# One more seven-product chunk in the second column half of an output projection

## The chip, the cores and the metric

The kernel runs on one core of a Trainium2 chip. The metric is the device time of one execution in microseconds (us). The engines are TensorE (PE, with its weight loads shown as PEld), VectorE (DVE), ScalarE (ACT), GpSimd (POOL) and SyncE (SP); SP and POOL issue the DMAs.

## The reference

One decoder layer on 256 tokens with model width 2048, all in float32:

```python
proj = h @ w_in[l]                                   # q, k, v of 16 heads of 128
a_out = diff_attention(q_d, k_d, v_d, ...)           # 8 heads, two 64-wide sub-heads each
b_out = moba_attention(q_m, k_m, v_m, cos_m, sin_m)  # 8 heads; 256 tokens are one block
mix = jnp.concatenate([a_out, b_out], axis=-1) @ w_out[l]
h = layer_norm(DEEPNORM_ALPHA * h + mix, ln1_g[l], ln1_b[l])
f = conv_ffn(h, w_up[l], conv_w[l], conv_b[l], w_down[l])   # width 5632
h = layer_norm(DEEPNORM_ALPHA * h + f, ln2_g[l], ln2_b[l])
```

The change touches `@ w_out` (2048 x 2048), its preparation during the attention, and the first `layer_norm`.

## The kernel before

**Stages.** Weights are streamed once, in items of a `stream` list, and the order of every engine's work is the order in which the code is written. There are 16 items for v, 32 for q and k (a q item and a k item for each head, called steps 0 to 31 here, counted from `first_q`), 16 for the output projection (from `first_o`; steps 32 to 47 in the same count), then 88 for gate and up, then the down projection. Each weight tile is loaded as float32 (`raw`, by SP at L179), then split into a rounded part `hi` (ACT, L203) and a remainder `lo` (DVE, L205; some remainders go by ACT L201 and a POOL DMA L202). A product of blocks is three matmuls: hi with hi, lo with hi, hi with lo. All of these are recorded at L303.

**Attention steps.** For each head there are: the Square of the previous head's output and its scale (`out_norm`: ACT L482, DVE L483 `ss`, POOL L484, then ACT L491), the scores' maxima (`scores`: DVE L412, and L416 `nm`), the exponentials (`exps`: ACT L426), the probabilities (`probs`: DVE L434 `rs` to L441), and on PE the transposes of the probabilities (`probs_t`: L450). The transposes stand in PE's queue between the q and k matmuls.

**Output projection.** The columns are handled in two halves (`half` 0 and 1), each with eight chunks `j` of 256 rows of `w_out`. A chunk is eight block products for its two row blocks and two token blocks, or 24 matmuls of 128x512. Some chunks use a Strassen-like scheme of seven products, or 21 matmuls. Its weight sums are either made on the spot (`mm_seven`; in half 0 chunk 6, in half 1 chunk 3), or made ahead (`mm_ready`; the list `READY`). Both also need sums of the two activation blocks (`act_sums` on DVE, `act_sums_split` on ACT and DVE). In half 0 chunks 3, 5 and 4 are in `READY`; two chunks of the down projection (`"d"`) are there as well. The second of these, `APART`, has its own tiles.

**Sums made ahead.** `READY_AT` gives five steps for each chunk: the DMA load of the weights into `prep` tiles (`ready_load`, SP, L832 or L835), two pairs of DVE sums (`ready_sums`: L852 and L853, then L855 and L856), and two remainders (`ready_lo`: DVE L881). Half a step behind each pair of sums stands the rounding (`ready_hi`: ACT L875), and half a step behind each remainder the store of both parts to a DRAM tile `tsums` (`ready_store`: POOL L888, L889). The chunk `STAYS` is kept on the chip and isn't stored. Before the output projection needs a stored chunk, `ready_fetch` loads it into `oslot`. These calls are put into the stream's steps behind the attention's own, by `pending`. All chunks share two `prep` tiles in turn: the load of chunk c goes into the tile of the second sums of chunk c-1.

**Around the projection's end.** `o_shared` adds the products that several outputs share into `z` (DVE L1286), `z_piece` adds a finished bank to `z` and takes its statistics (L518, L521), `normed` normalises a piece of `z` (L1346), and PE transposes it (L1355). The first matmuls of gate and up need the transposed pieces.

```python
READY_AT = ((0, 3, 5, 7, 9), (8.5, 11, 13, 15, 17), (17.5, 20, 21, 22, 23), (23.5, 26, 27, 29, 34.5), (2.5, 5, 9, 13, 17))
...
for step, fn, j in ((x, ready_load, ()), (u[0], ready_sums, (0,)), (u[0] + 0.5, ready_hi, (0,)),
                    (u[1], ready_sums, (1,)), (u[1] + 0.5, ready_hi, (1,)), (u[2], ready_lo, (0,)),
                    (u[2] + 0.5, ready_store, (0,)), (u[3], ready_lo, (1,)), (u[3] + 0.5, ready_store, (1,))):
```

Of the kernel before, what the change touches and what calls it, by code (L numbers as in the profile page):

```python
# [11 lines left out]
F32 = mybir.dt.float32  # L12
# [4 lines left out]
P = 128  # L17
D = 2048
# [39 lines left out]
STAYS, APART = 3, 4  # L58

ORDER = {"v": (1, 0, 2, 3), "d": (0, 1, 2, 3), "o": (2, 0, 1, 3)}  # L60

# [18 lines left out]
def hymba_layer(ctx: ExitStack, tc: tile.TileContext, a: dict):  # L80
# [25 lines left out]
        stream.append(("q", h, 0, a["w_qk"][h, 0]))  # L106
        stream.append(("k", h, 0, a["w_qk"][h, 1]))
    for half in range(2):
        for j in range(8):
            stream.append(("o", half, j, a["w_o"][half, j]))  # L110
    for f in range(FT):

# [518 lines left out]


    gap = []

    def act_sums(i):
        kind, p, _, _ = stream[i]
        if kind == "d":
            return
        if kind == "o":
            j = 2 * stream[i][2]  # L640
            if "hraw" not in kept:
                kept["hraw"] = keep.tile([P, 4, S], F32, name="hraw", tag="four")
                kept["hsum"] = [keep.tile([P, S], F32R, name=n, tag=t) for n, t in (("hh", "cos_m"), ("hl", "sin_m"))]
            x = kept["hraw"][:, 0:2]
            both = [heads[k, j // NDIFF][:, j % NDIFF:j % NDIFF + 2].bitcast(F32) for k in range(2)]
            DVE.tensor_tensor(x, *both, ALU.add)
# [177 lines left out]
    def ready_load(c):  # L824
        if c == 0:
            ready["w"] = [keep.tile([P, 2048], F32, name="prep", tag=x) for x in ("za", "zb")]
            ready["dram"] = dram.tile([len(READY), P, 8, 512], F32R, name="tsums")
        if c == APART:
            ready["apart"] = [keep.tile([P, 2048], F32, name="apart", tag=x) for x in ("mab", "mbb")]
        kind, p, n = READY[c]  # L830
        if kind == "o":
            SP.dma_start(ready_half(c, 0), a["w_o"][p, n])  # L832
            return
        for k in range(2):
            SP.dma_start(ready_half(c, 0)[:, k * 1024:k * 1024 + 1024],  # L835
                         a["w_d"][2 * p + 1 - k][:, n * 1024:(n + 1) * 1024])
# [435 lines left out]
    def o_shared(n, part):  # L1272

        if part == 0:
            kept["ou"] = [work.tile([P, 512], F32, name="tf", tag="m1") for _ in range(2)]
            kept["ou"].append(work.tile([P, 512], F32, name="u", tag="sh", bufs=1))
        a, b, c = kept["ou"]
        if part == 0:
            ACT.activation(a, MO[n][1], AF.Copy)
            DVE.tensor_tensor(b, MO[n][6], a, ALU.add)  # L1280
            DVE.tensor_tensor(c, MO[n][7], b, ALU.add)
        adds = (((0, 1, MO[n][5], ALPHA), (1, 1, MO[n][5], ALPHA), (0, 0, a, ALPHA)) if part == 0 else
                ((0, 1, b, 1.0), (1, 0, c, ALPHA), (1, 1, c, 1.0)))
        for t, c, src, alpha in adds:
            y = z[:, t, (2 * n + c) * 512:(2 * n + c + 1) * 512]
            DVE.scalar_tensor_tensor(y, y, alpha, src, op0=ALU.mult, op1=ALU.add)  # L1286

    last = range(first_u - PAIRED, first_u)
    for i in range(first_o, last[0]):
# [4 lines left out]
        if i == last[0] - 1:  # L1294
            both = Two(*(keep.tile([P, 2, 1024], F32R, name="both", tag=x) for x in ("biga", "bigb")), 2)
            split(first_u + 1, 0, both)
            split(first_u + 1, 1, both)
        if i == first_o:
            oslot()
            ready_fetch(first_o + 3, [kept["oslot"][:, 0:8]], POOL)  # L1300
        if seven(i) or ready_of(i) is not None:
            for kk in range(2):
                aparts[i, kk] = head(0, 2 * stream[i][2] + kk), head(1, 2 * stream[i][2] + kk)
            if seven(i):
                mm_seven(i)
            else:
                mm_ready(i, (1, 2, 3, 4, 5, 7, 6))
        elif i == last[0] - 1:
            for kk in range(2):
                mm_o(i, kk, 0)  # L1310
        else:
            if not ahead:
                mm_o(i, 0, 1)
            mm_o(i, 0, 0)
            if ahead:
                mm_o(i, 1, 1)
            middle(i)
# [4 lines left out]
        n, j = stream[i][1:3]
        if i == first_o + 1:
            z0 = keep.tile([P, 1, D], F32, name="z", tag="za")
# [707 lines left out]
```

## Time and profile before

| | |
|---|---|
| median of 3 runs | 1100.79 us (1100.35 to 1100.85) |
| profiled execution, its own time | 1100.75 us |
| span of that execution | 1099.0 us |
| PE busy | 1092.2 us (99%) |
| DVE busy | 964.9 us (88%) |
| ACT busy | 739.5 us (67%) |
| bytes moved | 305.86 MB |

The span is the time from the first to the last instruction; the execution's own time is 1.75 us longer. All instants below are us from the span's start. A row of the trace gives the start, the duration, the engine, the line, the operation, its output and inputs, and, in square brackets, how long the engine had been idle before it and what ended that. A q or k step lasts about 6.4 us (the second chunk's sums, of steps 11 and 13, start at 161.22 and 174.05 us), and the output projection runs from about 300 us to 387 us.

### The profile page before, as it was taken

To read this page: it belongs to the slowest core of one execution; us is meant where nothing else is said; L and a number is where in the kernel's file an instruction comes from. 1 tells how busy PE (TensorE), PEld (TensorE's weight loads), DVE (VectorE), ACT (ScalarE), POOL (GpSimd) and SP (SyncE) were. 2 spreads that over 40 slices of the span, in tenths; PEclk is the share of its full clock that TensorE was granted. 3 is DMA by queue.
4 is the path that set the end of the run, shared out by engine and by line. 5 is a ranking of instruction groups with operands and counts; after the bars stand their busy time and mean duration, and the time that the engine had idled before them with its cause. 6 is when DMAs were issued, how large, how long until landed. Compare 5 with 4: busy or idle time off the path is not lost.

```text
span 1099.0 us, 16343 instructions
## 1 busy us (share of the span) xinstructions
PE 1092.2 (99%) x5879; PEld 942.4 (86%) x5879; DVE 964.9 (88%) x1652; ACT 739.5 (67%) x1199; POOL 88.2 (8%) x125
## 2 busy tenths in 40 slices
PE   9999999999999999999999999999999999999998
PEld 6888888888888898888888888888888888888886
DVE  6988899898789979888999989998899988999887
ACT  5766677766556586666666767676776767777563
POOL 0100111110000000000000000000000001000003
PEclk9999999999999999999999999999999999999999
DMA  9888898988788557988988889898898899888683
GB/s 328 275 279 270 271 328 271 321 257 261 248 321 259 206 204 228 290 275 267 310 278 287 282 295 335 295 316 296 278 275 282 316 317 293 290 286 266 232 323 123
DMA packets 73082, 305.86 MB, mean 278 GB/s; under 512 B 7604, under 2 KB 9640, under 8 KB 54440
## 3 DMA queue, kind: packets, MB, share of 16 engines
q1 hardware_dynamic: 58168, 242.67, 59.5%
q0 software_dynamic: 14400, 59.78, 23.0%
q10 hardware_dynamic: 432, 2.36, 0.6%
q8 instruction: 46, 0.75, 0.3%
q14 instruction: 36, 0.29, 0.1%
HBM read 245.49 MB, written 28.84 MB: 250 GB/s over the span
## 4 chain that ended last, share of the span: by engine, by line
PE 99%; DMA 0%; ACT 0%; SPq 0%; issue 0%; ACTq 0%
PE bank L303 98%; PE bank L450 0%; DMA raw<-in_w_v 0%; PE bank L1355 0%; PE bank L497 0%; ACT z L1961 0%; ACT hi L235 0%; PE bank L1394 0%; ACT z L1957 0%; SPq L165 0%; SPq L250 0%; PE bank L1946 0%; ACTq L1957 0%
## 5 line engine op out<-in xcount | busy, mean ns | idle before, releaser
L303 PE MATMUL bank<-h,hi 128*128 128x512 f32 x1376 | 480.9, 391 | 0.0
L303 PE MATMUL bank<-h,lo 128*128 128x256 f32 x1376 | 388.1, 282 | 0.0
L303 PEld LDWEIGHTS bank<-h,hi 128*128 128x128 f32 x1376 | 258.3, 188 | 54.3
L303 PEld LDWEIGHTS bank<-h,lo 128*128 128x128 f32 x1376 | 260.2, 189 | 3.7
L223 DVE TENSOR_TENSOR lo<-raw,hi 128x1024 fp32r<-128x1024 f32 x175 | 211.8, 1214 | 13.0 <-ACT hi L215 12.4
L215 ACT ACTIVATE hi<-raw 128x1024 fp32r<-128x1024 f32 x175 | 181.9, 1043 | 6.9 <-PE bank L303 6.9
L303 PE MATMUL bank<-x,hi 128*128 128x512 f32 x512 | 183.0, 398 | 0.0
L203 ACT ACTIVATE hi<-raw 128x1024 fp32r<-128x1024 f32 x121 | 124.9, 1045 | 33.6 <-PE bank L303 17.4
L205 DVE TENSOR_TENSOR lo<-raw,hi 128x1024 fp32r<-128x1024 f32 x105 | 124.3, 1206 | 24.1 <-ACT hi L203 23.8
L303 PE MATMUL bank<-x,lo 128*128 128x256 f32 x512 | 144.3, 282 | 0.0
L1014 ACT ACTIVATE tslot<-tf 128x512 fp32r<-128x512 f32 x144 | 88.7, 627 | 61.9 <-DVE tf L1676 27.0
L303 PEld LDWEIGHTS bank<-x,hi 128*128 128x128 f32 x512 | 96.2, 188 | 20.5 <-issue 1.0
L1017 DVE TENSOR_TENSOR tslot<-tf,tslot 128x512 fp32r<-128x512 f32 x144 | 97.7, 688 | 11.4 <-ACT tslot L1014 10.5
L1481 ACT ACTIVATE ub<-bank 128x512 f32<-128x512 f32 x86 | 50.8, 591 | 72.0 <-PE bank L303 71.9
L303 PEld LDWEIGHTS bank<-x,lo 128*128 128x128 f32 x512 | 96.8, 189 | 0.2
L303 PE MATMUL bank<-hi,x 128*128 128x512 f32 x192 | 51.7, 391 | 0.6 <-ACT hi L235 0.6
L1622 POOL DMA_DIRECT2D rslot<-raw x17 | 14.9, 879 | 436.9 <-ACT sp L1020 436.9
L303 PE MATMUL bank<-tslot,more 128*128 128x512 f32 x192 | 49.1, 391 | 0.0
L591 ACT ACTIVATE gc<-ub,vec 128x256 f32<-128x256 f32 x43 | 25.8, 599 | 30.9 <-DVE ub L1490 30.9
L1490 DVE TENSOR_TENSOR ub<-ub 128x256 f32<-128x256 f32 x86 | 36.2, 420 | 11.8 <-ACT ub L1481 11.8
L303 PE MATMUL bank<-tslot,sp 128*128 128x512 f32 x180 | 45.0, 391 | 0.0
L303 PEld LDWEIGHTS bank<-hi,x 128*128 128x128 f32 x192 | 35.8, 188 | 8.8 <-ACT hi L235 1.5
(354 smaller groups left out, 1739.4 us busy)
## 6 DMA issues: line engine op xcount, KB each, us to landing
raw<-in_w_u SPq DMA_DIRECT2D x88, 1024.0 KB, 6.9
raw<-in_w_qk SPq DMA_DIRECT2D x32, 1024.0 KB, 6.2
raw<-in_w_d SPq DMA_DIRECT2D x48, 512.0 KB, 8.6
rows<-in_w_d SPq DMA_DIRECT2D x38, 512.0 KB, 5.1
raw<-in_w_v SPq DMA_DIRECT2D x28, 512.0 KB, 8.9
raw<-in_w_o SPq DMA_DIRECT2D x13, 1024.0 KB, 7.8
rslot<-raw POOLq DMA_DIRECT2D x17, 768.0 KB, 7.0
dparts<-rslot SPq DMA_DIRECT2D x38, 256.0 KB, 8.1
```

The lines of the kernel that those rows point to most:

```text
L203: ACT.activation(hi[:, s], t[:, x:y], AF.Copy)
L205: DVE.tensor_tensor(lo[:, s], t[:, x:y], hi[:, s].bitcast(F32), ALU.subtract)
L215: ACT.activation(hi[:, 0:w], t[:, half * 1024:half * 1024 + w], AF.Copy)
L223: DVE.tensor_tensor(lo[:, 0:w], t[:, half * 1024:half * 1024 + w], hi[:, 0:w].bitcast(F32), ALU.subtract)
L303: PE.matmul(out, lhsT, rhs, start=start, stop=stop)
L591: ACT.activation(gates[f], g, AF.Identity, bias=vec[:, C_CB + f:C_CB + f + 1], scale=vec[:, C_W + 2 * FT + f:C_W + 2 * FT + f + 1])
L1014: ACT.activation(side["t"][:, 0, j], f, AF.Copy)
L1017: DVE.tensor_tensor(side["t"][:, 1, j], f, side["t"][:, 0, j].bitcast(F32), ALU.subtract)
L1481: ACT.activation(t.rearrange("p j t -> p (j t)"), up_bank(i), AF.Copy)
L1490: DVE.tensor_tensor(u[:, 0], u[:, 0], u[:, 1], ALU.add)
L1622: POOL.dma_start(side["r"][:, 1], w[:, 0:3], accum_op=ALU.add)
```

## The change

A sixth chunk, `("o", 1, 5)`, joins `READY`: chunk 5 of half 1 now takes seven products by `mm_ready` and no longer eight. In half 1 it is worked ahead of chunk 4 rather than behind it (`O_ORDER`). The sums of the activations of chunks 3 and 5, which half 0 makes, stay in their tiles (`held`) and are used again in half 1, so `act_sums` does nothing there. These sums are written in smaller pieces (128x256 and 128x128 rather than 128x512 and 128x256), and in other tiles. In `READY_AT` the chunks stand closer: the second chunk's sums move from steps 11 and 13 to 10.5 and 12, its remainders from 15 and 17 to 13.5 and 15; the third chunk's load moves from 17.5 to 15.5 and its first sums from 20 to 17; the new chunk takes 21.5 to 26, and `STAYS` starts at 27.5 rather than 23.5. Weights for the prepared `"o"` chunks are loaded in two DMAs rather than one, except for `STAYS`. The new chunk's sums are fetched in four DMAs of 0.5 MB at `first_o + 7`. Two of the six `z` additions of half 1 (`o_shared(1, 1)`) move behind the first token half's `normed`, and a remainder split of the next stage moves between two `z_piece` calls.

```diff
-READY = (("o", 0, 3), ("o", 0, 5), ("d", PT - 2, 0), ("o", 0, 4), ("d", PT - 1, 0))
+READY = (("o", 0, 3), ("o", 0, 5), ("d", PT - 2, 0), ("o", 1, 5), ("o", 0, 4), ("d", PT - 1, 0))
-READY_AT = ((0, 3, 5, 7, 9), (8.5, 11, 13, 15, 17), (17.5, 20, 21, 22, 23), (23.5, 26, 27, 29, 34.5), (2.5, 5, 9, 13, 17))
+READY_AT = ((0, 3, 5, 7, 9), (8.5, 10.5, 12, 13.5, 15), (15.5, 17, 18, 19, 20), (21.5, 23.5, 24.5, 25, 26),
+            (27.5, 29.5, 31, 30.5, 34.5), (2.5, 5, 9, 13, 17))
+SUMS_AT = ((5, 0), (5, 1), (4, 0), (6, 0))
+O_ORDER = (range(8), (0, 1, 2, 3, 5, 4, 6, 7))
...
     def act_sums(i):
+        if kind == "o" and p == 1:
+            sums[i] = held[n]
+            return
...
-            SP.dma_start(ready_half(c, 0), a["w_o"][p, n])
+            for x, y in ((1024, 2048), (0, 1024)) if c != STAYS else ((0, 2048),):
+                SP.dma_start(ready_half(c, 0)[:, x:y], a["w_o"][p, n][:, x:y])
...
-    for j, step in enumerate((first_q + 28, first_o + 2.5)):
+    for j, step in enumerate((first_q + 30, first_o + 2.5)):
         extra.setdefault(step, []).insert(0, (ready_here, (j, "hi")))
...
-        adds = (((0, 1, MO[n][5], ALPHA), (1, 1, MO[n][5], ALPHA), (0, 0, a, ALPHA)) if part == 0 else
-                ((0, 1, b, 1.0), (1, 0, c, ALPHA), (1, 1, c, 1.0)))
+        adds = (((0, 1, MO[n][5], ALPHA), (1, 1, MO[n][5], ALPHA), (0, 0, a, ALPHA), (0, 1, b, 1.0)) if part == 0 else
+                ((1, 0, c, ALPHA), (1, 1, c, 1.0)))
...
-            split(first_u + 1, 1, both)
...
-            for part in range(2):
+            for part in range(2 - n):
                 at(i + 1 + part / 2, o_shared, n, part, rank=0)
         if i == first_o + 7:
             SP.dma_start(z[:, 1, 1024:], a["x"][:, 1, 1024:])
+            ready_fetch(first_o + 12, [kept["oslot"][:, 8:16]])
...
     z_piece(0, 2, bank[4], 1, 512, 1.0)
+    split(first_u + 1, 1, both)
...
     for c in range(4):
         normed(0, mv, rstd, c)
+    o_shared(1, 1)
     for j in range(2):
         split_lo(first_u, j)
```

Below, the same places in the order of the instructions, with the line numbers of each kernel; in the changed kernel they are 4 to 12 higher (L875 is L884 there, L482 is L486, L426 is L430, L881 is L890).

ACT at the second chunk's first rounding (step 12, about 158 to 165 us). `on` is the attention output, `e` the scores, `prep` the chunk's weights; `m` is q and k before the rotation. Before:

```order
L482 ACTIVATE on,ss<-bank_78 128x128 x2
L316 ACTIVATE m_1547<-bank_72 128x256
L201 ACTIVATE lo<-raw 128x1024
L203 ACTIVATE hi<-raw 128x1024
L491 ACTIVATE on<-bank_78,rr 128x128 x2
L203 ACTIVATE hi<-raw 128x1024
L426 ACTIVATE e,sm<-e,nm 128x128
L426 ACTIVATE e,sm<-e,nm 128x256
L426 ACTIVATE e,sm<-e,nm 128x128
L426 ACTIVATE e,sm<-e,nm 128x256
L875 ACTIVATE prep<-prep 128x1024
```

After:

```order
L486 ACTIVATE on,ss<-bank_78 128x128 x2
L320 ACTIVATE m_1551<-bank_72 128x256
L205 ACTIVATE lo<-raw 128x1024
L207 ACTIVATE hi<-raw 128x1024
L884 ACTIVATE prep<-prep 128x1024
L495 ACTIVATE on<-bank_78,rr 128x128 x2
L207 ACTIVATE hi<-raw 128x1024
L430 ACTIVATE e,sm<-e,nm 128x128
L430 ACTIVATE e,sm<-e,nm 128x256
L430 ACTIVATE e,sm<-e,nm 128x128
L430 ACTIVATE e,sm<-e,nm 128x256
```

The rounding of `prep` moved from behind the four exponentials to ahead of the scaling L491 (now L495). Its second rounding, at the next head, moved in the same way from behind the exponentials to ahead of that head's Square, together with its sums on DVE, which moved from behind `nm` to ahead of `ss`.

SP from the second chunk's load to the fourth's. `x9` is nine DMAs in a row. Before:

```order
L832 DMA prep<-in_w_o 128x2048
L179 DMA raw<-in_w_qk 128x2048 x9
L835 DMA prep<-in_w_d 128x1024 x2
L179 DMA raw<-in_w_qk 128x2048 x6
L832 DMA prep<-in_w_o 128x2048
```

After:

```order
L841 DMA prep<-in_w_o 128x1024 x2
L183 DMA raw<-in_w_qk 128x2048 x7
L844 DMA prep<-in_w_d 128x1024 x2
L183 DMA raw<-in_w_qk 128x2048 x6
L841 DMA prep<-in_w_o 128x1024 x2
```

The load of the third chunk from `in_w_d` moved ahead of two loads of q and k weights. The load behind it is the new chunk's.

DVE behind the seventh head's `nm` (step 17, about 200 us). L852 and L853 are sums of a chunk. Before:

```order
L416 TENSOR_SCALAR nm<-mx 128x4
L881 TENSOR_TENSOR prep<-prep 128x1024
L881 TENSOR_TENSOR apart<-apart 128x1024
L205 TENSOR_TENSOR lo<-raw,hi 128x1024
L434 RECIPROCAL rs<-sm 128x4
```

After:

```order
L420 TENSOR_SCALAR nm<-mx 128x4
L861 TENSOR_TENSOR prep<-prep 128x512
L862 TENSOR_TENSOR prep<-prep 128x512
L890 TENSOR_TENSOR apart<-apart 128x1024
L209 TENSOR_TENSOR lo<-raw,hi 128x1024
L438 RECIPROCAL rs<-sm 128x4
```

The remainder of `prep` made room for the two sums of the third chunk, which need its load. Its second sums stand in the next head ahead of `ss`, and its first remainder behind that head's `nm`; before, nothing of a chunk stood there.

DVE at the end of the projection, where the first token half is normalised (376.67 us). Before:

```order
L528 TENSOR_SCALAR ve<-mv 128x1
L1346 TENSOR_SCALAR z<-z,mv,rstd 128x512 x4
L223 TENSOR_TENSOR lo<-raw,hi 128x1024 x2
L1369 CAST h_3584<-hf 128x4x128
L1370 TENSOR_TENSOR h_3584<-hf,h_3584 128x4x128
L518 SCALAR_TENSOR_TENSOR z<-z,bank_77 128x512
```

After:

```order
L532 TENSOR_SCALAR ve<-mv 128x1
L1358 TENSOR_SCALAR z<-z,mv,rstd 128x512 x4
L1296 SCALAR_TENSOR_TENSOR z<-z,u 128x512 x2
L227 TENSOR_TENSOR lo<-raw,hi 128x1024 x2
L1381 CAST h_3592<-hf 128x4x128
L1382 TENSOR_TENSOR h_3592<-hf,h_3592 128x4x128
L522 SCALAR_TENSOR_TENSOR z<-z,bank_77 128x512
```

The two additions to `z` came in behind the first `normed`.

More of the change, by code (lines that the diff above doesn't have):

```diff
@@ L54 @@
 SEVEN = {"v": ((5,), range(1, 8, 3)), "d": ((), ()), "o": ((6,), (3,))}
-READY = (("o", 0, 3), ("o", 0, 5), ("d", PT - 2, 0), ("o", 0, 4), ("d", PT - 1, 0))
-READY_AT = ((0, 3, 5, 7, 9), (8.5, 11, 13, 15, 17), (17.5, 20, 21, 22, 23), (23.5, 26, 27, 29, 34.5), (2.5, 5, 9, 13, 17))
-STAYS, APART = 3, 4
+READY = (("o", 0, 3), ("o", 0, 5), ("d", PT - 2, 0), ("o", 1, 5), ("o", 0, 4), ("d", PT - 1, 0))
+READY_AT = ((0, 3, 5, 7, 9), (8.5, 10.5, 12, 13.5, 15), (15.5, 17, 18, 19, 20), (21.5, 23.5, 24.5, 25, 26),
+            (27.5, 29.5, 31, 30.5, 34.5), (2.5, 5, 9, 13, 17))
+STAYS, APART = 4, 5
+SUMS_AT = ((5, 0), (5, 1), (4, 0), (6, 0))
+O_ORDER = (range(8), (0, 1, 2, 3, 5, 4, 6, 7))
 ORDER = {"v": (1, 0, 2, 3), "d": (0, 1, 2, 3), "o": (2, 0, 1, 3)}
@@ L108, in hymba_layer @@
     for half in range(2):
-        for j in range(8):
+        for j in O_ORDER[half]:
             stream.append(("o", half, j, a["w_o"][half, j]))
@@ L633, in hymba_layer @@
     gap = []
+    held = {}
     def act_sums(i):
-        kind, p, _, _ = stream[i]
+        kind, p, n, _ = stream[i]
         if kind == "d":
+            return
+        if kind == "o" and p == 1:
+            sums[i] = held[n]
             return
@@ L641, in act_sums @@
             if "hraw" not in kept:
[L642 to L646, printed above, removed]
+                kept["hraw"] = [keep.tile([P, S], F32, name="hraw", tag=t) for t in ("cos_m", "sin_m")]
+                kept["hsum"] = keep.tile([P, 4, S], F32R, name="hsum", tag="four")
+            x = kept["hraw"]
+            for c in range(2):
+                both = [heads[k, j // NDIFF][:, j % NDIFF + c].bitcast(F32) for k in range(2)]
+                DVE.tensor_tensor(x[c], *both, ALU.add)
         else:
@@ L650, in act_sums @@
         f = [f[:, 0], f[:, 1]]
-        if kind == "o":
-            DVE.tensor_tensor(f[0], x[:, :, P:2 * P], x[:, 0].rearrange("p (t c) -> p t c", c=P), ALU.subtract)
-            x = [x[:, k] for k in range(2)]
         a11, a21, a12, a22 = (x[k][:, t * P:(t + 1) * P] for k in range(2) for t in range(2))
-        if kind != "o":
-            DVE.tensor_tensor(f[0][:, 0], a21, a11, ALU.subtract)
-            DVE.tensor_tensor(f[0][:, 1], a22, a21, ALU.subtract)
+        DVE.tensor_tensor(f[0][:, 0], a21, a11, ALU.subtract)
+        DVE.tensor_tensor(f[0][:, 1], a22, a21, ALU.subtract)
         DVE.tensor_tensor(f[1][:, 0], f[0][:, 1], a11, ALU.add)
@@ L662, in act_sums_split @@
     def act_sums_split(i):
-        if stream[i][0] == "d":
+        kind, p, n, _ = stream[i]
+        if kind == "d" or kind == "o" and p == 1:
             return
@@ L670, in act_sums_split @@
                 gap.append(work.tile([P, 8], F32, name="gap", bufs=1))
-            if i == first_o + 5 or i == first_o + 4 and j == 0:
+            if kind == "o" and (n, j) in SUMS_AT:
                 if "osum" not in kept:
                     kept["osum"] = keep.tile([P, 2304], F32R, name="osum", tag="e")
-                o = 512 * (j if i == first_o + 5 else 2)
+                o = 512 * SUMS_AT.index((n, j))
                 hi, lo = (kept["osum"][:, o + S * k:o + S * k + S] for k in range(2))
-            elif j == 0 and stream[i][0] == "o":
-                hi, lo = kept["hsum"]
+            elif kind == "o" and n == 3:
+                hi, lo = (kept["hsum"][:, 2 * j + k] for k in range(2))
             elif j == 0:
@@ L687, in act_sums_split @@
         sums[i] = out
+        if kind == "o":
+            held[n] = out
     blocks = {}
@@ L903, in ready_fetch @@
         if len(tiles) == 1:
-            for j in range(2):
-                queue.dma_start(tiles[0][:, 4 * j:4 * j + 4].bitcast(F32), src[:, 4 * j:4 * j + 4].bitcast(F32))
+            w = 2 if i == first_o + 12 else 4
+            for j in sorted(range(0, 8, w), key=lambda j: j % 4):
+                queue.dma_start(tiles[0][:, j:j + w].bitcast(F32), src[:, j:j + w].bitcast(F32))
             ready[i] = [(tiles[0][:, j], tiles[0][:, 4 + j]) for j in range(4)]
@@ L1307, in hymba_layer @@
                 mm_ready(i, (1, 2, 3, 4, 5, 7, 6))
+            if i == last[0] - 2:
+                split(i + 3, 1)
         elif i == last[0] - 1:
@@ L1321, in hymba_layer @@
             done(i)
[L1322 removed]
+        n, j = stream[i][1], (i - first_o) % 8
         if i == first_o + 1:
[L1324 removed]
+            z0 = keep.tile([P, 1, D], F32, name="z", tag="zb")
             SP.dma_start(z0[:, 0], a["x"][:, 0])
@@ L1327, in hymba_layer @@
         if i == first_o + 2:
-            z = Two(z0, keep.tile([P, 1, D], F32, name="z", tag="zb"), 1)
+            z = Two(z0, keep.tile([P, 1, D], F32, name="z", tag="za"), 1)
             SP.dma_start(z[:, 1, 0:1024], a["x"][:, 1, 0:1024])
-        if j == max(SEVEN["o"][n] + tuple(x[2] for x in READY if x[:2] == ("o", n))):
-            for part in range(2):
+        if j == max(O_ORDER[n].index(x) for x in SEVEN["o"][n] + tuple(x[2] for x in READY if x[:2] == ("o", n))):
+            for part in range(2 - n):
                 at(i + 1 + part / 2, o_shared, n, part, rank=0)
```

## The prediction

> **What bounds the kernel now.** I read the busy times on the page first, then the waits of PE, then the stretches of the attention, then single rows at the places that the change touches.
>
> ```profile
> PE 1092.2 (99%) x5879; PEld 942.4 (86%) x5879; DVE 964.9 (88%) x1652; ACT 739.5 (67%) x1199; POOL 88.2 (8%) x125
> PE bank L303 <- DVE idle L1075: 1.2, 1, 1.2
> PE bank L303 <- ACT hi L235: 0.6, 1, 0.6
> 120.00:210.00 90.00, 90.00 (x562) 79.57 (x563) 82.96 (x202) 66.74 (x158) 17.16 (x25) 1.00 0.91 294
> 210.00:310.00 100.00, 100.00 (x579) 88.56 (x578) 82.35 (x183) 61.25 (x125) 10.02 (x14) 1.00 0.84 275
> ```
>
> PE is busy 99% of the span, and its waits behind its first matmul are 1.8 us in all (the two rows: how long in total, how often, the longest). So a gain comes only from fewer matmuls, and whatever makes PE wait is added in full. The stretches (PE, PEld, DVE, ACT and POOL busy, granted clock, DMA share, GB/s) cover the attention: PE is never idle, but DVE is busy 83 of 90 us there and the DMA engines 91%, so little room is left for moving work. The question is how far PE's operands are ahead at the transposes L450, which need the probabilities of DVE.
>
> **The gain.** Chunk 5 of half 1 goes from 24 matmuls to 21. The first and last start of 24 such matmuls in the projection:
>
> ```profile
> 368.43 0.39 PE L303 MATMUL bank<-hi,mh 128*128 128x512 f32 x1
> 373.64 0.39 PE L303 MATMUL bank<-hi,ml 128*128 128x512 f32 x1
> ```
>
> (373.64 - 368.43) / 23 = 0.227 us each, so the change removes 3 x 0.227 = 0.7 us. The activation sums and splits that fall away in half 1 lie on DVE and ACT beside PE, which waits for neither there: worth 0.
>
> **Second chunk, first rounding.** DVE's, ACT's, PE's and SP's rows:
>
> ```profile
> 159.50 0.16 DVE L483 TENSOR_SCALAR ss<-ss 128x2 f32<-128x2 f32 x1
> 161.22 0.69 DVE L852 TENSOR_TENSOR prep<-prep 128x512 f32<-128x512 f32 x1
> 166.12 0.48 DVE L441 SCALAR_TENSOR_TENSOR e<-e,rs 128x256 f32<-128x256 f32 x1
> 161.81 1.08 ACT L203 ACTIVATE hi<-raw 128x1024 fp32r<-128x1024 f32 x1
> 162.76 0.42 ACT L426 ACTIVATE e<-e,nm 128x128 f32<-128x128 f32 x1
> 164.52 1.06 ACT L875 ACTIVATE prep<-prep 128x1024 fp32r<-128x1024 f32 x1
> 166.98 0.49 PE L450 MATMUL bank<-ident,e 128*128 128x128 f32 x3
> 147.10 0.33 SPq L832 DMA_DIRECT2D prep<-in_w_o x1
> DMA to landing us min/median/max: 13.4/13.4/13.4
> ```
>
> The probabilities end at 166.60 and are used at 166.98: 0.4 us to spare. The weights land at 147.10 + 13.4 = 160.5. The sums now stand ahead of `ss` (159.50), so DVE stands still until 160.5, adds until about 161.8 and has pushed all of the head's DVE work back by 2.3 us. On ACT the rounding follows at 161.8, takes 0.95 (161.81 to 162.76 is the step of one such operation), then L491 0.5 and one `hi` 0.95: the exponentials start at 164.2 rather than 162.76, 1.4 us late. Less 0.4 to spare, PE waits 1.0 us. Bounds: 0.95 - 0.4 = 0.55 if the load costs nothing, 1.8 if the data are there only at 161.22, when the sums ran before. I take 1.0, by the rows' own landing.
>
> **Second chunk, second rounding.**
>
> ```profile
> 170.07 2.35 DVE L205 TENSOR_TENSOR lo<-raw,hi 128x1024 fp32r<-128x1024 f32 x2
> 178.18 0.18 DVE L434 RECIPROCAL rs<-sm 128x4 f32<-128x4 f32 x1 [0.45 <-ACT e L426]
> 179.63 0.48 DVE L441 SCALAR_TENSOR_TENSOR e<-e,rs 128x256 f32<-128x256 f32 x1
> 170.96 0.28 ACT L482 ACTIVATE on<-bank 128x128 f32<-128x128 f32 x1 [2.01 <-PE bank L303]
> 171.82 0.38 ACT L316 ACTIVATE m<-bank 128x256 f32<-128x256 f32 x1 [0.24 <-PE bank L303]
> 175.33 1.06 ACT L203 ACTIVATE hi<-raw 128x1024 fp32r<-128x1024 f32 x1 [0.71 <-PE bank L303]
> 181.02 0.49 PE L450 MATMUL bank<-ident,e 128*128 128x128 f32 x3
> ```
>
> The sums come behind one remainder (170.07 + 1.13) and end at 172.5. The rounding waits for them and ends at 173.5, and Square stands behind it: 2.5 us late, of which ACT's idle 0.24 + 0.71 takes up 0.95. On DVE the first remainder of `prep` takes the place of the sums behind `nm`. So the exponentials are 1.55 us late, against 181.02 - 180.11 = 0.9 to spare; but DVE comes in 0.4 us later against PE than before, since the first wait has used that up. PE waits 1.55 - 0.9 + 0.4 = 1.0 us (bounds 0 if that 0.4 is regained and ACT fits the rounding into its 2.01 us of idle time, 2.0 if none of its later idle time helps).
>
> **Third chunk's load.** The load (two DMAs of 512 KB) now goes out behind the raw load of 195.47, and its sums stand behind the `nm` that starts at 200.33:
>
> ```profile
> 195.47 2.53 SPq L179 DMA_DIRECT2D raw<-in_w_qk  x2
> 206.59 2.80 SPq L835 DMA_DIRECT2D prep<-in_w_d  x2
> DMA to landing us min/median/max: 4.6/8.7/13.4
> 200.41 1.22 DVE L881 TENSOR_TENSOR prep<-prep 128x1024 fp32r<-128x1024 f32 x1
> 204.53 0.18 DVE L434 RECIPROCAL rs<-sm 128x4 f32<-128x4 f32 x1 [0.53 <-ACT e L426]
> 205.99 0.48 DVE L441 SCALAR_TENSOR_TENSOR e<-e,rs 128x256 f32<-128x256 f32 x1
> 207.37 0.49 PE L450 MATMUL bank<-ident,e 128*128 128x128 f32 x3
> raw<-in_w_qk SPq DMA_DIRECT2D x32, 1024.0 KB, 6.2
> ```
>
> The second of the two can be issued at about 195.5 + 0.4 + 1.4 = 197.3. With 8.7 us, the median of `prep`'s DMAs, it lands at 206.0; by the queue, the raw load lands 6.2 us behind 195.47 and 1 MB more at the 294 GB/s of this stretch takes 3.6 us: 205.3. DVE reached this place at 200.41. Behind the waiting sums stand the remainders of `apart` and `raw`, then `rs` and the probabilities, and for these PE waits. From 205.3: 4.9 us late, plus 0.2 (two sums for one remainder), less 0.53 of idle time and 0.9 to spare (207.37 - 206.47): PE waits 3.7 us. Bounds: with 4.6 us the load lands at 201.9 and 0.3 is left; with 13.4 us it is 9. I take 3.7, nearer to the median. The Trainium skill, DMA: Bandwidth & Descriptors, section Anatomy of one DMA, gives about 2.0 us plus bytes / 436e3 for a DMA of GpSimd's path, for 512 KB an estimate of 3.2 us; by it the load would be there at 200.5 and this term would be 0. The trace disagrees: its shortest is 4.6 us. The raw loads that stand behind this load on SP go out up to 2.8 us later (the two issues take that long); they are split a step or more after they land, so I count nothing for it, but if that cover is gone the next splits wait as this one does, which the bound of 9 holds. POOL's stores of the second chunk are issued a step earlier; POOL is busy 17 of 90 us and DVE's `ss` releases it, so 0.
>
> **Third chunk, second sums.**
>
> ```profile
> 209.94 2.35 DVE L205 TENSOR_TENSOR lo<-raw,hi 128x1024 fp32r<-128x1024 f32 x2
> 211.34 0.28 ACT L482 ACTIVATE on<-bank 128x128 f32<-128x128 f32 x1 [2.01 <-PE bank L303]
> 218.97 0.49 DVE L441 SCALAR_TENSOR_TENSOR e<-e,rs 128x256 f32<-128x256 f32 x1
> 220.36 0.82 PE L450 MATMUL bank<-ident,e 128*128 128x128 f32 x6
> ```
>
> As with the second chunk: sums until 209.94 + 1.13 + 1.3 = 212.4, rounding until 213.4, Square 2.0 us late, now with no idle time on ACT behind it. Less 0.9 to spare, 1.1; with the 0.9 that the wait before it used up, PE waits 2.0 us (bounds 0.5, where DVE's idle time takes up part, and 2.5).
>
> **New chunk and `STAYS`.** From step 21 on only one set of sub-heads is left in a head, and there is more to spare:
>
> ```profile
> 244.60 0.55 DVE L444 TENSOR_SCALAR e<-e,rs 128x128 f32<-128x128 f32 x2
> 247.07 0.49 PE L450 MATMUL bank<-ident,e 128*128 128x128 f32 x3
> ```
>
> 247.07 - 245.15 = 1.9 us cover the 1.0 us of a rounding or the 1.3 us of two sums. I take 0 (bounds 0 and 2, if a load is late here as above). The extra traffic, 1 MB read, 2 MB stored and 2 MB fetched, less 0.25 MB that chunk 5 needs no more, is 4.75 MB, or 16 us of the DMA engines at 294 GB/s, spread over some 200 us.
>
> **The two additions to `z`.**
>
> ```profile
> 366.84 1.29 DVE L1286 SCALAR_TENSOR_TENSOR z<-z,u 128x512 f32<-128x512 f32 x2
> 386.32 0.55 DVE L1346 TENSOR_SCALAR z<-z,mv,rstd 128x512 f32<-128x512 f32 x1 [0.67 <-POOL rstd L529]
> 386.92 0.55 PE L1355 MATMUL bank<-ident,z 128*128 128x128 f32 x3
> ```
>
> They take 1.2 us (two starts 0.6 apart) and now stand in DVE's chain behind the first `normed`. That chain runs to the second `normed` at 386.32 with no idle time but the 0.67 for `rstd`, which waits for it. PE transposes its result 0.05 us behind its end, so all of it arrives: 1.2 us (bounds 0 and 1.2). The other moves (split loads, four fetches, the split between two `z_piece` calls) cost 0: the fetches have five projection chunks to land in, and the split only changes places with work that waits for PE.
>
> **Sum.** -0.7 + 1.0 + 1.0 + 3.7 + 2.0 + 0 + 1.2 = +8.2 us. Against the profiled execution (1100.75, its span 1099.0 and 1.75 around it) that is 1108.95; its time is 0.04 from the median, so I say 1109.0.
>
> **Rivals.** *The stalls don't come* (same): the moved work fits into idle time, and only the matmuls count: 1100.75 - 0.7 = 1100.1. For it speaks that DVE has 7 us idle in 120 to 210; against it that 0.4 and 0.9 us are to spare where 1.4 to 2.0 are added. It decides if the late exponentials stay below these. Even then it can hardly be faster by more than 0.7 + 1.8 = 2.5 us, all PE's waits. Chance 0.14.
>
> *The third chunk's load is in time:* its term falls to 0.3 and the next to 1.1: 1100.75 + 3.9 = 1104.7. The 4.6 us speak for it, the 91% DMA share against. Chance 0.20.
>
> *The DMA engines become the bound:* the loads of the new chunk and of `STAYS` are late too, each by 3.7 + 0.9 less 1.9 to spare, 2.7 us: 1109.0 + 5.4 = 1114.4. Chance 0.08. Here the skill's TensorE: Matmul & The Clock Gate, section on the HAM clock gate, speaks against the change too: an idle window of about 3.4 us halves the clock for about as long, an estimate of 1.7 us more at the longest wait. No row shows such a wait; the granted clock is 1.00 throughout.
>
> **How the numbers follow.** My own case has 0.58 and by its bounds 1106 to 1113. With the rivals, the range for 8 times in 10 is 1103.0 to 1113.5, which leaves out the first rival and the third. A measurement can tell about 0.2%, 2.2 us, from no change: slower 0.84, same 0.14 (first rival), faster 0.02.
>
> **What would show it.** PE waits for DVE's `e` at L450 near 167, 181, 207 (the longest, with DVE waiting for a DMA into `prep`) and 220 us, and for `z` at the end of the projection; none between 230 and 380 us. I am wrong if DVE never waits for `prep` near 200 us, if PE's waits are below 2 us in sum, or if new waits stand at the fetched sums.

## The result, and the profile after

The changed kernel took 1108.26 us (median of 6 runs, 1107.46 to 1108.95) against 1100.82 us for the kernel before (6 runs, 1100.35 to 1101.6): 7.4 us more, a ratio of 1.0068 with a 95% interval of 1.0055 to 1.0081. The profiled execution took 1107.46 us, with a span of 1105.7 us, so 6.7 us more than the one before. One execution each of the experiments with the second chunk's packing, with the old steps and with the late additions took between 2825 and 3895 us, and their medians leave it out.

From its page and its views of waits (how long in total, how often, the longest) and stretches:

```profile
PE 1094.1 (99%) x5876; PEld 941.7 (85%) x5876; DVE 967.2 (87%) x1660; ACT 741.8 (67%) x1199; POOL 90.5 (8%) x129
PE bank L454 <- DVE e L445: 3.9, 7, 0.9
PE bank L1367 <- DVE z L1358: 1.2, 1, 1.2
PE bank L501 <- ACT on L495: 0.2, 1, 0.2
DVE prep L861 <- DMA prep<-in_w_d: 3.2, 1, 3.2
120.00:210.00 90.00, 87.92 (x546) 76.80 (x544) 79.60 (x193) 65.87 (x157) 17.10 (x25) 1.00 0.90 288
210.00:310.00 100.00, 97.99 (x566) 85.69 (x567) 85.45 (x186) 61.49 (x121) 12.16 (x18) 1.00 0.85 279
```

PE ran 3 matmuls fewer and now waits for DVE at the transposes of the probabilities and once at the transposes of `z`, and a little for ACT at one pair of transposes of `on` (L501); before, none of these waits was there. In the attention's two stretches PE is idle for 2.1 and 2.0 us, where it was never idle. The granted clock is 1.00 in both.

How much each place cost is read from PE's starts: the start of a matmul in the changed kernel less the start of the same matmul before says how late PE is there, and a place costs by how much this grows across it. PE's rows of the changed kernel, at the waits and, for the third place, also ahead of and behind it:

```profile
167.31 0.44 PE L454 MATMUL bank<-ident,e 128*128 128x128 f32 x2 [0.35 <-DVE e L445]
182.05 0.33 PE L454 MATMUL bank<-ident,e 128*128 128x128 f32 x1 [0.58 <-DVE e L445]
209.03 0.28 PE L307 MATMUL bank<-x,lo 128*128 128x256 f32 x1
210.21 0.33 PE L454 MATMUL bank<-ident,e 128*128 128x128 f32 x1 [0.90 <-DVE e L445]
210.99 0.44 PE L454 MATMUL bank<-ident,e 128*128 128x128 f32 x2 [0.46 <-DVE e L445]
211.19 0.48 PE L307 MATMUL bank<-x,hi 128*128 128x512 f32 x1
221.33 0.44 PE L501 MATMUL bank<-ident,on 128*128 128x128 f32 x2 [0.23 <-ACT on L495]
225.20 0.33 PE L454 MATMUL bank<-ident,e 128*128 128x128 f32 x1 [0.66 <-DVE e L445]
393.65 0.66 PE L1367 MATMUL bank<-ident,z 128*128 128x128 f32 x4 [1.22 <-DVE z L1358]
```

Before, the two L307 rows stood at 207.25 and 207.62. So PE is 1.78 us late ahead of the third place and 3.57 behind it: the place cost 1.8, more than the 0.90 and 0.46 in the brackets. A bracket counts from the modelled end of the row ahead (209.03 + 0.28 = 209.31), while in the kernel before the transposes started 0.12 us behind the start of that row (207.25 and 207.37); and the brackets leave out part of what a wait between two transposes costs.

Read in this way, the changed kernel is 0.30 us early ahead of the first place, from its start. Then it is late by 0.29 behind the first place, 1.78 behind the second, 3.58 behind the third and 5.93 behind the fourth: they cost 0.59, 1.49, 1.80 and 2.35. Of the fourth, 0.45 lies at the transposes of `on` (221.33) that stand ahead of those of the probabilities (225.20). Until 309 us another 0.28 is added, and by the second token half's `z` another 0.52, which is 1.21 for the wait for `z` less 0.69 for the three matmuls. From there the last long stretch of matmuls runs 6.73 us later than before.

### The profile page after: what moved, and what is told of

It reads as the page before. It is cut to its first block, busy times and chain, and to the rows that moved or that the text cites. A ratio compares the mean times of both kernels' runs of the same rounds, so it can differ in the third digit from the quotient of the medians.

```text
span 1105.7 us, 16376 instructions
## 1 busy us (share of the span) xinstructions
PE 1094.1 (99%) x5876; PEld 941.7 (85%) x5876; DVE 967.2 (87%) x1660; ACT 741.8 (67%) x1199; POOL 90.5 (8%) x129
## 3 DMA queue, kind: packets, MB, share of 16 engines
q0 software_dynamic: 14976, 61.87, 23.5%
## 4 chain that ended last, share of the span: by engine, by line
PE 91%; DVE 5%; ACT 2%; DMA 1%; issue 1%; POOL 0%; SPq 0%; DVEq 0%; ACTq 0%
PE bank L307 90%; DVE lo L209 1%; DMA prep<-in_w_d 1%; DMA lo<-raw 1%; ACT hi L207 1%; PE bank L454 0%; ACT e L430 0%; DVE e L445 0%; ACT prep L884 0%; ACT lo L205 0%; DVE e L444 0%; DVE lo L227 0%; DVE st L525 0%; DVE hraw L655 0%; DVE oslot L741 0%
## 5 line engine op out<-in xcount | busy, mean ns | idle before, releaser
L307 PE MATMUL bank<-h,hi 128*128 128x512 f32 x1376 | 480.9, 390 | 0.0
L307 PE MATMUL bank<-h,lo 128*128 128x256 f32 x1376 | 387.9, 282 | 0.0
L307 PEld LDWEIGHTS bank<-h,hi 128*128 128x128 f32 x1376 | 258.2, 188 | 54.6
L307 PEld LDWEIGHTS bank<-h,lo 128*128 128x128 f32 x1376 | 259.9, 189 | 3.7
L307 PE MATMUL bank<-x,hi 128*128 128x512 f32 x512 | 183.0, 398 | 0.0
L307 PE MATMUL bank<-x,lo 128*128 128x256 f32 x512 | 144.2, 282 | 0.0
L307 PEld LDWEIGHTS bank<-x,hi 128*128 128x128 f32 x512 | 96.1, 188 | 20.6 <-issue 1.0
L1027 DVE TENSOR_TENSOR tslot<-tf,tslot 128x512 fp32r<-128x512 f32 x144 | 97.7, 688 | 11.5 <-ACT tslot L1024 10.5
L307 PEld LDWEIGHTS bank<-x,lo 128*128 128x128 f32 x512 | 96.8, 189 | 0.2
L307 PE MATMUL bank<-hi,x 128*128 128x512 f32 x192 | 51.9, 392 | 0.0
L307 PE MATMUL bank<-tslot,more 128*128 128x512 f32 x192 | 49.1, 391 | 0.0
L307 PE MATMUL bank<-tslot,sp 128*128 128x512 f32 x180 | 45.0, 391 | 0.0
L307 PEld LDWEIGHTS bank<-hi,x 128*128 128x128 f32 x192 | 36.2, 189 | 8.2 <-ACT hi L239 0.8
```

What stands on the lines that cost most here:

```text
L307: PE.matmul(out, lhsT, rhs, start=start, stop=stop)
L1027: DVE.tensor_tensor(side["t"][:, 1, j], f, side["t"][:, 0, j].bitcast(F32), ALU.subtract)
```

## The experiments

All but the last three ran beside the kernel before, whose median was 1100.62 us with the experiments on the second chunk's packing, the small load, the old steps and the earlier additions, 1100.74 with the later rounding, the later `STAYS` and the late additions alone, and 1101.1 with the new chunk's sums later. The losses are worked out as above, from one profiled execution of each kernel (us). The first column includes the transposes of `on` near 164 us, the fourth those near 217; the columns are named by the kernel before's times.

| kernel | 164 to 167 | 181 | 207 | 217 to 220 | rest to 309 | end of projection |
|---|---|---|---|---|---|---|
| the changed kernel | 0.59 | 1.49 | 1.80 | 2.35 | 0.28 | 0.52 |
| second chunk's packing alone | 1.91 | 1.48 | 0 | 0 | 0 | 0 |
| small third load | 2.28 | 1.48 | 0 | 1.41 | 0 | 0.56 |
| rounding later | 0.99 | 0.10 | 3.81 | 0 | 0 | 0.84 |
| additions to `z` earlier | 0.58 | 1.47 | 3.07 | 2.33 | 0 | -0.27 |
| old steps | 0 | 0 | 0 | 0 | 6.37 | 0.52 |
| old steps, `STAYS` later | 0 | 0 | 0 | 0 | 2.61 | 0.29 |
| old steps, new chunk's sums later too | 0 | 0 | 0 | 0 | 0.33 | -0.11 |
| additions to `z` late, alone | 0 | 0 | 0 | 0 | 0 | 1.17 |
| the changed kernel, three more traces | 0.57 to 0.58 | 1.47 | 1.90 to 2.06 | 2.31 | 0 to 0.17 | 0.49 to 0.51 |

**The second chunk's packing alone**, in the kernel before:

```diff
-READY_AT = (..., (8.5, 11, 13, 15, 17), ...
+READY_AT = (..., (8.5, 10.5, 12, 13.5, 15), ...
```

> The kernel before with one edit: the second chunk's steps (8.5, 11, 13, 15, 17) become (8.5, 10.5, 12, 13.5, 15). Theory (the packed steps push sums and rounding ahead of the attention's work): PE waits at the transposes near 167 and 181 us, 0.7 + 1.3 = 2.1 us in all, 1102.9 us, and no other wait, since the third chunk is where it was. Rival (what costs is the traffic of the extra chunk, which is absent here): 1100.8 us, no wait.

Measured: 1104.0 us, ratio 1.0029 (1.0018 to 1.0041). The two waits are there and no others, without the extra chunk, so the rival falls. The first place cost 1.91 rather than 0.7. The rows of DVE and ACT show why; the last row is DVE's in the changed kernel:

```profile
161.04 0.69 DVE L852 TENSOR_TENSOR prep<-prep 128x512 f32<-128x512 f32 x1 [1.72 <-DMA tsums<-prep]
162.25 0.16 DVE L483 TENSOR_SCALAR ss<-ss 128x2 f32<-128x2 f32 x1
162.37 1.07 ACT L875 ACTIVATE prep<-prep 128x1024 fp32r<-128x1024 f32 x1 [1.20 <-DVE prep L853]
159.21 0.68 DVE L861 TENSOR_TENSOR prep<-prep 128x512 f32<-128x512 f32 x1
```

The sums write over the part of `prep` that the chunk before is storing to DRAM, and here DVE waited 1.72 us for that store. The chunk's own load came little sooner: it is one DMA here, issued at 147.06 us, and landed 13.0 us later, at 160.1. In the changed kernel the load is two DMAs, issued from 145.10 on, and its sums started at 159.21 without a wait for either. So this kernel's price is not quite the changed kernel's. But with the same two DMAs, two of the experiments below waited there too: how much the first place costs changes from run to run with a landing.

**The third chunk's load cut to 32 of 1024 columns**, in the changed kernel; the sums of that chunk are then made from old data.

```diff
+            w = 32 if c == 2 else 1024
-            SP.dma_start(ready_half(c, 0)[:, k * 1024:k * 1024 + 1024],
-                         a["w_d"][2 * p + 1 - k][:, n * 1024:(n + 1) * 1024])
+            SP.dma_start(ready_half(c, 0)[:, k * 1024:k * 1024 + w],
+                         a["w_d"][2 * p + 1 - k][:, n * 1024:n * 1024 + w])
```

> The changed kernel, with the third chunk's two loads cut to 32 of their 1024 columns, so that the sums of that chunk are made from old data; all instructions stay where they are. Theory (the wait near 200 us is for this load's landing): the DVE wait of 3.2 us goes, with it PE's 2.4 us at 210 us and 0.9 of the 1.75 us at 225 us: 1108.3 - 3.3 = 1105.0 us. Rival (the added DVE and ACT work is what is late there, the load is just the last of several): less than 1 us is gained, over 1107.3 us.

Measured: 1105.15 us (1104.58 to 1107.08). DVE's wait in the changed kernel, and in this one:

```profile
202.20 0.17 DVE L420 TENSOR_SCALAR nm<-mx 128x4 f32<-128x4 f32 x1
205.52 0.69 DVE L861 TENSOR_TENSOR prep<-prep 128x512 f32<-128x512 f32 x1 [3.15 <-DMA prep<-in_w_d]
209.01 0.17 DVE L438 RECIPROCAL rs<-sm 128x4 f32<-128x4 f32 x1
```

```profile
204.85 0.17 DVE L420 TENSOR_SCALAR nm<-mx 128x4 f32<-128x4 f32 x1
205.30 0.69 DVE L862 TENSOR_TENSOR prep<-prep 128x512 f32<-128x512 f32 x1 [0.29 <-DMA prep<-in_w_d]
208.94 0.18 DVE L438 RECIPROCAL rs<-sm 128x4 f32<-128x4 f32 x1
```

From `nm` to the sums it is 0.45 us rather than 3.3, and PE loses nothing near 207 us rather than 1.80. So that loss is the load's landing and not the added work. At the fourth place, 1.41 of the 2.35 us stay: most of that place's loss is its own. The profiled execution, at 1107.08 the longest of the five, lost 2.28 us at the first place, where DVE waited 1.05 for the store and 0.75 for a load.

**The roundings of the second and third chunk later**, in the changed kernel:

```diff
-... (u[0] + 0.5, ready_hi, (0,)), (u[1], ready_sums, (1,)), (u[1] + 0.5, ready_hi, (1,)), ...
+... (u[0] + (1 if c in (1, 2) else 0.5), ready_hi, (0,)), (u[1], ready_sums, (1,)),
+    (u[1] + (1.5 if c in (1, 2) else 0.5), ready_hi, (1,)), ...
```

> The changed kernel with the roundings (ACT) of the second and third chunk moved behind the exponentials again or, for the third chunk's first, behind the q and k copies; sums, remainders, loads stay where the change put them. Theory (at 167, 181 and 225 us it is the rounding ahead of Square or of the exponentials that is late): those waits go, 0.7 + 1.3 + about 1.4 us, the wait for the third chunk's load stays: about 1104.9 us. Rival (the sums on DVE ahead of ss are what is late): the waits stay, 1108.3 us.

Measured: 1106.34 us, ratio 1.0052 (1.0039 to 1.0064), between the two. ACT's rows of the changed kernel, at the second place and at the fourth, show the rounding waiting 4.1 us for the sums while Square (L486) stands behind it; then PE's and DVE's rows of this experiment:

```profile
173.33 1.06 ACT L884 ACTIVATE prep<-prep 128x1024 fp32r<-128x1024 f32 x1 [4.10 <-DVE prep L865]
174.30 0.26 ACT L486 ACTIVATE on<-bank 128x128 f32<-128x128 f32 x1
217.02 1.07 ACT L884 ACTIVATE prep<-prep 128x1024 fp32r<-128x1024 f32 x1 [4.11 <-DVE prep L865]
```

```profile
181.86 0.58 PE L454 MATMUL bank<-ident,e 128*128 128x128 f32 x3
225.12 0.60 PE L454 MATMUL bank<-ident,e 128*128 128x128 f32 x4
160.15 0.69 DVE L861 TENSOR_TENSOR prep<-prep 128x512 f32<-128x512 f32 x1 [0.71 <-DMA tsums<-prep]
205.17 0.69 DVE L861 TENSOR_TENSOR prep<-prep 128x512 f32<-128x512 f32 x1 [3.63 <-DMA prep<-in_w_d]
```

The waits of the second and the fourth place are gone (0.10 and 0 lost), that for `on` near 221 us with them: the rounding ahead of Square was the cause there, though the sums on DVE stand where they stood. At the first place 0.99 stayed, where DVE waited 0.71 us for the store; what the rounding alone costs there is not shown. At 207 us the loss grew to 3.81, which the expectation missed. DVE waited 3.63 us for the load, not 3.15, since it came to the sums earlier; and behind PE's wait there the clock went down. The stretches (the clock is the third number from the right), and the first matmul of some pairs of 512 and 256 columns, during it and behind it:

```profile
205.00:211.00 6.00, 4.17 (x26) 3.35 (x25) 5.69 (x12) 3.09 (x6) 0.54 (x1) 1.00 1.03 322
211.00:215.00 4.00, 4.00 (x16) 3.37 (x15) 3.89 (x7) 1.44 (x2) 0.00 (x0) 0.57 0.88 287
211.25 0.49 PE L307 MATMUL bank<-x,hi 128*128 128x512 f32 x1
...
213.03 0.63 PE L307 MATMUL bank<-x,hi 128*128 128x512 f32 x1
...
213.67 0.63 PE L307 MATMUL bank<-x,hi 128*128 128x512 f32 x1
...
214.90 0.39 PE L307 MATMUL bank<-x,hi 128*128 128x512 f32 x1
...
216.91 0.40 PE L307 MATMUL bank<-x,hi 128*128 128x512 f32 x1
...
217.26 0.39 PE L307 MATMUL bank<-x,hi 128*128 128x512 f32 x1
```

A pair took 0.64 us (213.03 to 213.67) where it takes 0.35 behind it, at a granted clock of 0.57 over the 4 us. The six pairs from 211.25 to 214.90 took 3.65 us instead of 6 x 0.35 = 2.1, so about 1.6 of the 3.81 us is the clock's, and 2.2 the wait's. The 0.84 at the end of the projection, 0.3 more than in the changed kernel, is not explained.

**The old steps for the second and third chunk**, with the extra chunk squeezed in behind them:

```diff
-READY_AT = ((0, 3, 5, 7, 9), (8.5, 10.5, 12, 13.5, 15), (15.5, 17, 18, 19, 20), (21.5, 23.5, 24.5, 25, 26),
+READY_AT = ((0, 3, 5, 7, 9), (8.5, 11, 13, 15, 17), (17.5, 20, 21, 22, 23), (23.5, 25.5, 26, 26.5, 27),
             (27.5, 29.5, 31, 30.5, 34.5), (2.5, 5, 9, 13, 17))
```

> The changed kernel with the old steps for the second and third chunk (8.5, 11, 13, 15, 17 and 17.5, 20, 21, 22, 23); the new chunk is packed into 23.5, 25.5, 26, 26.5, 27, where more is to spare, and STAYS is as in the changed kernel. Theory: the four waits between 160 and 230 us go; left are -0.7 for the matmuls, +1.2 for the additions to z, and 0 to 2 for the packed new chunk: 1101.3 to 1103.3 us. Rival (the extra traffic or the extra chunk itself costs the time): it stays above 1106 us.

Measured: 1108.2 us (1106.54 to 1109.38), ratio 1.0068 (1.0054 to 1.0082). The total is the rival's, but not its place:

```profile
277.10 0.33 SPq L841 DMA_DIRECT2D prep<-in_w_o  x1
288.21 0.69 DVE L861 TENSOR_TENSOR prep<-prep 128x512 f32<-128x512 f32 x1 [5.95 <-DMA prep<-in_w_o]
289.96 0.74 PE L454 MATMUL bank<-ident,e 128*128 128x128 f32 x3 [4.43 <-DVE e L448]
```

Until 272 us the transposes stand within 0.1 us of where they stood before: the four waits are gone with the extra chunk in place. Then one late load, that of `STAYS`, costs as much as all four (6.37 against 6.23 us). SP waited 3.3 us for the store of the new chunk before it issued this load at 277.10; DVE came to the sums 5.2 us later and could start them only at 288.21, 11 us behind the issue. Behind the wait the clock went down here too: 0.57 from 290 to 294 us, as long as in the experiment with the roundings, and 1.6 us are lost by it. This was my own spacing, which repeats the changed kernel's fault in another place.

**The same, with the sums of `STAYS` later**, and the additions to `z` ahead of the last `z` pieces (their edit stands below):

```diff
-            (27.5, 29.5, 31, 30.5, 34.5), ...
+            (27.5, 31, 32, 32, 34.5), ...
-    for j, step in enumerate((first_q + 30, first_o + 2.5)):
+    for j, step in enumerate((first_q + 31.5, first_o + 2.5)):
```

> As the experiment with the old steps for the second and third chunk, but the sums of STAYS 1 to 1.5 steps later (31 and 32 rather than 29.5 and 31, its first rounding at 31.5, its remainder at 32), so that its load has 1.5 steps more to land, and the two additions to z ahead of the last z pieces. Theory (no cost but late loads, rounding ahead of exponentials, and the additions): no wait from 120 to 380 us, -0.7 for the matmuls, +0.4 for the additions: 1100.3 us. Rival (the extra chunk's traffic or work costs something wherever it stands): 1102 us or more.

Measured: 1101.25 us, ratio 1.0005 (0.9997 to 1.0014). That load's wait is gone. In the profiled execution, the longest of them at 1103.54, the new chunk's load was late by 2.85 us and PE waited 2.2 us near 262, which the expectation did not have.

**The same, with the new chunk's sums half a step later too**, and `STAYS` behind them:

```diff
-..., (23.5, 25.5, 26, 26.5, 27), (27.5, 31, 32, 32, 34.5), ...
+..., (23.5, 26, 26.5, 27, 27.5), (28.5, 31.5, 32.5, 32.5, 34.5), ...
-    for j, step in enumerate((first_q + 31.5, first_o + 2.5)):
+    for j, step in enumerate((first_q + 32, first_o + 2.5)):
```

> As the experiment with STAYS later, but the new chunk's sums are made half a step later (26, 26.5, 27, 27.5 rather than 25.5, 26, 26.5, 27) and STAYS at 28.5, 31.5, 32.5, 32.5 with its first rounding at 32. Theory: with the sums behind the probabilities of the head near 260 us the load has about 5 us more to land, so PE's wait of 2.2 us there goes; left are -0.7 for the matmuls and +0.4 for the additions: 1100.4 us, which can't be told from before. Rival (the extra chunk brings a late load wherever its sums stand): a wait elsewhere, 1102 us.

Measured: 1101.27 us, ratio 1.0001 (0.9992 to 1.0010). PE's only wait from 100 to 420 us is

```profile
PE bank L1367 <- DVE z L1358: 0.6, 1, 0.6
```

That near 262 us is gone, and until 285 us every transpose stands within 0.1 us of before. With the whole extra chunk in place the kernel can't be told from before; it isn't faster either, as 0.31 us near 298 and the additions take up the 0.67 of the matmuls.

**The two additions to `z` earlier**, right behind the other additions of half 1, in the changed kernel:

```diff
-            for part in range(2 - n):
-                at(i + 1 + part / 2, o_shared, n, part, rank=0)
+            for part in range(2):
+                at(i + 1 + part * (1 - n) / 2, o_shared, n, part, rank=0)
...
-    o_shared(1, 1)
```

> The changed kernel with the two additions to z ahead of the last z pieces, right behind the other additions of half 1, rather than behind the first normed. Theory that only their place behind normed costs 1.2 us: 1107.1 us. Rival, by the trace of the changed kernel: DVE is idle for only 0.18 us between this place and the z piece that ends the first token half, so the additions push the first normed back by about 1.0 us and the gain is 0.2 us: 1108.1 us.

Measured: 1108.05 us, ratio 1.0069 (1.0056 to 1.0081), no different from the changed kernel's time. At their place, PE's wait is 0.4 us rather than 1.2 and the kernel gains 0.8 us, between what the two theories said; in the profiled execution the third chunk's load, for which DVE waited 4.43 us, gave that back. That the total meets the rival's 1108.1 is therefore chance.

**Only the additions to `z` late**, in the kernel before:

```diff
-        adds = ((..., (0, 0, a, ALPHA)) if part == 0 else
-                ((0, 1, b, 1.0), (1, 0, c, ALPHA), (1, 1, c, 1.0)))
+        adds = ((..., (0, 0, a, ALPHA), (0, 1, b, 1.0)) if part == 0 else
+                ((1, 0, c, ALPHA), (1, 1, c, 1.0)))
...
-            for part in range(2):
+            for part in range(2 - n):
...
         normed(0, mv, rstd, c)
+    o_shared(1, 1)
```

> The kernel before with only the two additions to z moved behind the first normed. Theory: all of their 1.2 us arrives at PE's transposes near 387 us: 1101.9 us. Rival (before, the additions were as much in the way ahead of normed, so moving them is neutral): 1100.7 us.

Measured: 1102.0 us, ratio 1.0011 (1.0002 to 1.0020), a difference of 1.3 us.

```profile
PE bank L1355 <- DVE z L1346: 1.2, 1, 1.2
379.18 1.29 DVE L1286 SCALAR_TENSOR_TENSOR z<-z,u 128x512 f32<-128x512 f32 x2
388.21 0.55 DVE L1346 TENSOR_SCALAR z<-z,mv,rstd 128x512 f32<-128x512 f32 x1 [0.67 <-POOL rstd L529]
388.81 0.66 PE bank L1355 x4
```

The one wait is theirs, 1.2 us, as long as the two additions.

**The changed kernel three times more**, for its traces alone, since the profiled execution was its shortest run:

> The changed kernel once more, for its trace alone. Theory (the runs above 1107.46 us have a stretch of about 3.4 us at a granted clock near 0.57 behind one of the waits for the third chunk's load, as the experiment with later roundings showed behind a wait of 1.4 us): such a stretch stands behind 210 us in a run near 1109 us, at 1.6 us lost. Rival (it is the landing of the load or of the store alone): the clock is 1.00 throughout and the difference stands in DVE's waits for prep near 160 and 205 us.

> The same kernel again, with the same two expectations: a slow stretch behind the wait at 210 us, or longer waits of DVE for prep at a granted clock of 1.00.

> The same kernel a third time, with the same two expectations.

Measured: 1107.79, 1108.30 and 1108.01 us. The clock is 1.00 at all the waits, so the slow stretch explains none of these. The rival holds in part: the third place cost 2.01, 1.90 and 2.06 us rather than 1.80, with DVE's waits for that load between 3.25 and 3.40 us rather than 3.15. Most of the rest lies ahead of the change's first place, where these runs are between 0.08 us ahead of the trace of before and 0.62 behind it, and the first profiled execution was 0.30 ahead. So the four waits, the 0.5 at the end and the start give the spread of the runs that were traced to within 0.3 us, the rest of which lies behind 389 us; the two runs near 1108.95 were not traced.

## Why the prediction was right

It said 1109.0 us, and 1108.26 was measured; all five waits came at the places named, one for `on` near 221 us came besides, and no rival held. Step by step, with the loss in the profiled execution:

- **The matmuls**, -0.7: -0.69, and hidden nowhere. The reading of what more could be gained was wrong: the 1.2 us (L1075) of the 1.8 us of PE's waits stand ahead of its first matmul, which starts at 1.19 us, so only 0.6 lie behind it.
- **Second chunk, first rounding**, 1.0: 0.59, and 0.57 to 2.28 over the profiled executions with that packing. The forecast had the sums wait until 160.5 us for a load issued at 147.10. In the changed kernel the load goes out in two DMAs from 145.10 on, and the sums ran at 159.21 without a wait: what came true is the lower bound, 0.55, where the load costs nothing. The store of the chunk before, which I did not count, sets this place too: 0.7 to 1.7 us of DVE's wait in three other kernels.
- **Second chunk, second rounding**, 1.0: 1.49 (1.47 to 1.49 in the six other traces that kept it). That the rounding ahead of Square is the cause is shown: without it 0.10 is left. The bound of 2.0, with no idle time of ACT regained, is as near as what I took.
- **Third chunk's load**, 3.7: 1.80 (1.80 to 2.06 in four traces of the changed kernel), the term most off. The landing was well placed: 205.3 was worked out, and it landed at 205.40. But I compared it with DVE's arrival in the kernel before (200.41). By then the changed kernel was 1.8 us late itself, so DVE came at 202.4 and waited 3.15 us rather than 4.9. With 3.15 the rest of the step comes out: 3.15 + 0.2 - 0.53 - 0.9 = 1.9. With the additions earlier it cost 3.07 at a clock of 1.00, as the load landed 8.65 us after its second DMA and not 7.76: the landing differs between executions.
- **Third chunk, second sums**, 2.0: 2.35, of which 0.45 at the transposes of `on`. I put 1.1 of it down to the rounding and 0.9 to the wait ahead of it. Without that wait 1.41 is left, without the rounding 0: the rounding's part was a little larger, and the load handed on 0.9, as was worked out.
- **New chunk and `STAYS`**, 0: 0.28 in the changed kernel. In two other spacings PE waited 2.2 and 4.4 us in one wait, both above my upper bound of 2: a late load there costs more than I allowed.
- **The additions to `z`**, 1.2: 1.2, shown alone in the kernel before.

The sum of the terms was 8.2; the places cost 7.0 in the profiled execution, of which its start gave 0.3 back, and the median of the runs lost 7.4. That the total is so near is partly luck, because the errors go both ways: -1.9 at the third place and -0.4 at the first, +0.5 at the second, +0.35 at the fourth and +0.3 behind it. In the changed kernel the load landed 7.8 us after its second DMA was issued (205.4 - 197.6). The estimate of 3.2 us for 512 KB that the prediction took from the Trainium skill, DMA: Bandwidth & Descriptors, section Anatomy of one DMA, is for GpSimd's path and does not give the landing of this load, which SP issues among other transfers.

```profile
197.08 1.05 SPq L844 DMA_DIRECT2D prep<-in_w_d  x2
197.64 7.76 DMA prep<-in_w_d
```

## What to carry to other kernels

Where one engine is busy for 99% of the time, as here, a saving of three matmuls was worth 0.69 us, and one rounding moved a step forward, from behind the work that it doesn't feed to ahead of it, cost 1.4 us: look at the order on every engine that feeds the busy one before counting what is saved. A wait for a transfer that stands in an engine's queue holds back everything behind it (here 3.15 us on DVE became 1.8 on PE); leave the transfer its longest landing, and remember that its buffer's last store has to land too. When several waits are added up, each must be taken against the timeline that the earlier ones have already pushed back.

## What was not expected of the hardware

The clock: in two of the experiments a stretch of about 3.5 to 4 us at a granted clock of 0.57 followed a wait of PE, once behind 4.43 us without work and once behind waits of 1.38 and 0.46 us near 210 us. Behind other waits it stayed at 1.00, even behind 2.17 us:

```profile
209.85 0.33 PE L454 MATMUL bank<-ident,e 128*128 128x128 f32 x1 [1.38 <-DVE e L445]
290.00:294.00 4.00, 4.00 (x14) 3.39 (x15) 3.89 (x8) 2.03 (x3) 0.00 (x0) 0.57 0.45 173
211.72 0.33 PE L454 MATMUL bank<-ident,e 128*128 128x128 f32 x1 [2.17 <-DVE e L445]
215.00:219.00 4.00, 4.00 (x28) 3.62 (x27) 3.93 (x6) 0.49 (x1) 0.00 (x0) 1.00 0.51 172
```

The first two rows are of the experiments with the later roundings and with the old steps, the last two of the one with the additions earlier. The prediction priced a halved clock at 1.7 us by the Trainium skill's TensorE: Matmul & The Clock Gate (section on the HAM clock gate), which asks for an idle window of about 3.4 us. The loss of about 1.6 us and the length of the stretch agree with it; that it can follow waits of 1.4 and 0.5 us does not, by these rows. Nor does the length of the break alone decide: between the matmuls ahead of and behind the transposes, PE ran nothing but transposes for 2.5 us in the first case (208.31 to 210.82) and for 3.3 us with the additions earlier (209.39 to 212.69), where the clock stayed at 1.00. What decides stays open. In the changed kernel itself no such stretch was seen in four traces.

The third chunk's load landed between 7.31 and 8.65 us after its second DMA was issued, in six executions of three kernels that send it from the same place, and the sums of the second chunk waited 0 to 1.05 us for a store in kernels that are alike up to there.
